# Nearest-neighbour upsampling: a fourth load for the last rows, and a first group copied by one engine

## The chip, the cores and the metric

The kernel runs on one core of a Trainium2 chip. The metric is the device time in microseconds (us) of one execution. A profile is one execution recorded by the hardware profiler; its span runs from the first instruction of the program to the last event that it records.

## The reference

```python
batch, channels, h, w = x.shape            # 16, 64, 64, 64, float32
new_h, new_w = (h * scale_factor, w * scale_factor)   # scale_factor = 2
...
        src_i = i // scale_factor
        src_j = j // scale_factor
        result[:, :, i, j] = x[:, :, src_i, src_j].copy()
```

Every input element is written four times: twice along the row and in two neighbouring rows. 16.78 MB are read, 67.11 MB are written, and nothing is computed.

## The kernel before

The 65,536 input rows of 64 numbers are spread over 128 partitions, 512 neighbouring rows in each (R = 512). One input row is 256 bytes in a partition, and becomes 256 numbers, 1 KB, of output (two output rows of 128).

One tile, `mem`, holds everything: 79 x 256 numbers of free room at its front, and behind it the whole input, `xt` (512 x 64 numbers). The groups of output rows are built in this tile and overwrite input that is used up: groups with an even number at the tile's start, groups with an odd number so that they end where the group's own input rows begin. Two groups that follow each other do not overlap, and a group overwrites the one two before it, or input already expanded. So the copies of a group wait for the store of the group two before it to land.

**Loads** (lines 192 to 195). Three DMAs issued on SyncE (SP), cut at rows 0, 32, 288 and 512 of each partition: 8 KB, 64 KB and 56 KB in each partition. `begin_before_barrier` (lines 13 to 33) takes the first `EARLY` instructions of SP in the body, which are these loads, and puts them ahead of the barrier that all engines pass at the start.

**Groups** (lines 204 to 216). `rows` gives nine groups of 54, 38, 54, 61, 54, 63, 63, 63 and 62 input rows. For each group VectorE (DVE in the profile, line 213) expands the first `kv` rows with a broadcast copy, ScalarE (ACT, line 214) the rest, and SP issues one store of the whole group (line 215), which waits for both:

```python
        kv = k - 1 if n == 0 else k * 5 // 8 & ~1
        nc.vector.tensor_copy(out=u[:, :kv], in_=expanded(r0, r0 + kv))
        nc.scalar.copy(out=u[:, kv:], in_=expanded(r0 + kv, r0 + k))
        nc.sync.dma_start(out=op[:, r0 : r0 + k, :], in_=u)
```

For groups 1 to 8 `kv` is five eighths of the rows, rounded down to an even number (22, 32, 38, 32, 38, 38, 38, 38). For group 0 it is all rows but one, 53, and ACT copies the one row. Group 0 needs rows 0 to 53, so loads 1 and 2. The second group overwrites input of group 0 and waits for VectorE's first copy.

All DMAs, loads and stores, are issued by SP on one hardware queue. Each increments one of eight semaphores, given out in turn; with three loads and nine stores there are twelve DMAs. `close_early` (lines 80 to 151) rewrites the end of the program: GpSimd waits for all semaphores but that of the last store and clears them, and SP waits for the last store alone. The loads are numbered 1 to 4 below, the groups and their stores 0 to 8.

Of the kernel before, what the change touches and what calls it, by code (L numbers as in the profile page):

```python
# [6 lines left out]

EARLY = 3  # L10


def begin_before_barrier(nc):
# [5 lines left out]
    sp = mybir.EngineType.SP  # L19
    loads = [i for i in body.instructions if i.engine == sp][:EARLY]  # L20
    for load in loads:
# [132 lines left out]
@with_exitstack  # L154
def kernel(
    ctx: ExitStack,
    tc: tile.TileContext,
    x: bass.AP,
    scale_factor: int,
    out: bass.AP,  # L160
):
    nc = tc.nc
    nc.at_finalize(begin_before_barrier)
    nc.at_finalize(close_early)
    P = nc.NUM_PARTITIONS
    s = int(scale_factor)
    B, C, H, W = x.shape
    R = B * C * H // P
    fdt = x.dtype

    xp = x.rearrange("b c h w -> (b c h) w").rearrange("(p r) w -> p r w", p=P)
    op = out.rearrange("b c (h hd) w -> (b c h) (hd w)", hd=s).rearrange(
        "(p r) w -> p r w", p=P
    )

    rows = [54, 38, 54, 61, 54, 63, 63, 63, 62]
    GROW = s * s
    FREE = 79
    WF = FREE * GROW * W
    assert sum(rows) == R
    mem_pool = ctx.enter_context(tc.tile_pool(name="mem", bufs=1))
    mem = mem_pool.tile([P, WF + R * W], fdt, name="mem")
    xt = mem[:, WF:].rearrange("p (r w) -> p r w", r=R)

    HEAD = 32
    cuts = [0, HEAD, R // 2 + HEAD, R]
    for lo, hi in zip(cuts, cuts[1:]):
        nc.sync.dma_start(out=xt[:, lo:hi], in_=xp[:, lo:hi])  # L195

    def expanded(r0, r1):
        return (
            xt[:, r0:r1].unsqueeze(2).unsqueeze(4).to_broadcast([P, r1 - r0, s, W, s])
        )  # L200

    r0 = 0
    before = (0, 0)
    for n, k in enumerate(rows):
        size = k * GROW * W
        at = 0 if n % 2 == 0 else WF + r0 * W - size
        assert at >= before[1] or at + size <= before[0]
        before = (at, at + size)
        u = mem[:, at : at + size].rearrange(
            "p (k a w b) -> p k a w b", k=k, a=s, w=W  # L210
        )
        kv = k - 1 if n == 0 else k * 5 // 8 & ~1
        nc.vector.tensor_copy(out=u[:, :kv], in_=expanded(r0, r0 + kv))  # L213
        nc.scalar.copy(out=u[:, kv:], in_=expanded(r0 + kv, r0 + k))  # L214
        nc.sync.dma_start(out=op[:, r0 : r0 + k, :], in_=u)  # L215
        r0 += k

# [34 lines left out]
```

## Time and profile before

| what | value |
|---|---|
| median of 3 runs | 197.13 us (197.12 to 197.15) |
| the profiled execution's own time | 196.92 us |
| its span | 195.6 us |
| busy: VectorE, ACT | 52.3 us, 42.1 us |
| DMA queue q1, share of 16 engines | 99.2% |
| bytes moved | 83.89 MB, mean 429 GB/s |
| VectorE's first copy, 53 rows | starts at 24.11 us, 14.29 us long |
| store 0 issued, landed | 38.48 us, 57.30 us |
| store 1 issued | 42.11 us |

In the profile's lines L213 is line 213 of the kernel before. A line of groups reads: line, engine, operation, output and input with shapes (partitions x elements), count, then the busy time in us and the mean duration of one in ns, then the idle time of that engine just before these instructions and what ended it. A line of the timeline reads: start, length, engine, line, operation, and in square brackets the idle time before it and what it waited for. The chain that ended last follows the work back from the last instruction, at each step to what released it. A row of DMA issues gives the count, the KB of one and the median time from issue to landing.

### The profile page before, as it was taken

The page shows a single profiled execution, that of the slowest core. Times are in us where ns is not written, and L with a number is a line of the kernel's source. Part 1 is how long each engine was busy: PE and PEld are TensorE (multiplying, and loading weights), DVE is VectorE, ACT ScalarE, POOL GpSimd, SP SyncE. Part 2 cuts the span into 40 slices and gives each one's busy share as a digit, 9 for nine tenths or more (in the row PEclk, how much of TensorE's full clock was granted, in tenths as well). Part 3 has the DMA queues.
Part 4 walks back from the last instruction along what each step waited for, and adds up shares of the span by engine and source line. Part 5 has one row for each costly group of instructions (what it writes and reads, how often), then busy time and mean ns, then how long its engine had stood idle before and what let it go on. Part 6 is the DMA issues. An engine that isn't in the chain of part 4 may idle for free.

```text
span 195.6 us, 102 instructions
## 1 busy us (share of the span) xinstructions
DVE 52.3 (27%) x9; ACT 42.1 (21%) x10; POOL 0.2 (0%) x4
## 2 busy tenths in 40 slices
DVE  0000099940026091053008204500540073000000
ACT  2000000160029700059500004970000073000000
POOL 0000000000000000000000000000000000000000
DMA  9999989889899989999999899999999999999994
GB/s 429 429 429 429 402 375 563 375 362 543 362 436 390 555 362 418 486 409 409 409 420 532 362 531 433 422 422 422 422 422 422 422 422 422 422 435 545 467 428 208
DMA packets 1728, 83.89 MB, mean 429 GB/s; under 512 B 192, under 2 KB 192, under 8 KB 192
## 3 DMA queue, kind: packets, MB, share of 16 engines
q1 hardware_dynamic: 1728, 83.89, 99.2%
HBM read 16.78 MB, written 67.11 MB: 429 GB/s over the span
## 4 chain that ended last, share of the span: by engine, by line
DMA 65%; ACT 11%; DVE 7%; SPq 0%; issue 0%; DVEq 0%; ACTq 0%
DMA out_dram<-mem 53%; DMA mem<-in_x_dram 12%; ACT mem L214 11%; DVE mem L213 7%; SPq L195 0%; DVEq L213 0%; ACTq L214 0%; SPq L215 0%
## 5 line engine op out<-in xcount | busy, mean ns | idle before, releaser
L213 DVE COPY mem<-mem 128x9728 f32<-128x9728 f32 (+3 forms) x9 | 52.3, 5818 | 110.9 <-DMA out_dram<-mem 86.8
L214 ACT COPY mem<-mem 128x6400 f32<-128x6400 f32 (+5 forms) x9 | 40.8, 4530 | 119.4 <-DMA out_dram<-mem 84.2
L214 ACT ACT_TABLE_LOAD x1 | 1.3, 1283 | 1.7 <-PEq L233 1.7
L233 POOL MEMSET const-bfloat16-1.0<- 128x1 bf16 x1 | 0.1, 102 | 0.0
L233 POOL MEMSET const-uint8-127<- 128x1 uint8 x1 | 0.1, 102 | 0.0
L233 POOL MEMSET const-float32-1.0<- 128x1 f32 x1 | 0.1, 99 | 0.0
L233 POOL MEMSET const-float32-0.0<- 128x1 f32 x1 | 0.1, 98 | 0.2 <-issue 0.2
## 6 DMA issues: line engine op xcount, KB each, us to landing
out_dram<-mem SPq DMA_DIRECT2D x3, 8064.0 KB, 32.4
out_dram<-mem SPq DMA_DIRECT2D x3, 6912.0 KB, 22.9
out_dram<-mem SPq DMA_DIRECT2D x1, 7936.0 KB, 32.3
out_dram<-mem SPq DMA_DIRECT2D x1, 7808.0 KB, 29.3
mem<-in_x_dram SPq DMA_DIRECT2D x1, 7168.0 KB, 40.1
out_dram<-mem SPq DMA_DIRECT2D x1, 4864.0 KB, 26.7
mem<-in_x_dram SPq DMA_DIRECT2D x1, 1024.0 KB, 4.7
mem<-in_x_dram SPq DMA_DIRECT2D x1, 23.6
```

Source lines behind the costliest of these rows:

```text
L213: nc.vector.tensor_copy(out=u[:, :kv], in_=expanded(r0, r0 + kv))
L214: nc.scalar.copy(out=u[:, kv:], in_=expanded(r0 + kv, r0 + k))
L233: nc = _bacc.Bacc("TRN2", target_bir_lowering=False, num_devices=1)
```

## The change

```diff
-EARLY = 3
+EARLY = 4
...
     HEAD = 32
-    cuts = [0, HEAD, R // 2 + HEAD, R]
+    TAIL = 8
+    cuts = [0, HEAD, R // 2 + HEAD, R - TAIL, R]
     for lo, hi in zip(cuts, cuts[1:]):
         nc.sync.dma_start(out=xt[:, lo:hi], in_=xp[:, lo:hi])
...
-        kv = k - 1 if n == 0 else k * 5 // 8 & ~1
+        kv = k if n == 0 else k * 5 // 8 & ~1
         nc.vector.tensor_copy(out=u[:, :kv], in_=expanded(r0, r0 + kv))
-        nc.scalar.copy(out=u[:, kv:], in_=expanded(r0 + kv, r0 + k))
+        if kv < k:
+            nc.scalar.copy(out=u[:, kv:], in_=expanded(r0 + kv, r0 + k))
         nc.sync.dma_start(out=op[:, r0 : r0 + k, :], in_=u)
```

Load 3 ends eight rows earlier (rows 288 to 503, 54 KB in each partition), and a fourth load brings rows 504 to 511 (2 KB in each partition). It too goes ahead of the barrier. Group 0 is copied by VectorE alone, 54 rows; ACT has no part in it, and store 0 waits for VectorE only. The rest is as before; the thirteenth DMA shifts by one which of the eight semaphores each store uses. In the built program ACT's table load, which stood ahead of its first copy without a wait, now stands behind a wait for loads 1 and 2.

## The prediction

> **What bounds the kernel now.** I read the page's share of busy time and its DMA rows first, then the chain that ended last, then the copies by form, and last the starts of single copies in the timeline. From the page:
>
> ```profile
> span 195.6 us, 102 instructions
> DVE 52.3 (27%) x9; ACT 42.1 (21%) x10; POOL 0.2 (0%) x4
> ...
> DMA packets 1728, 83.89 MB, mean 429 GB/s; under 512 B 192, under 2 KB 192, under 8 KB 192
> ...
> q1 hardware_dynamic: 1728, 83.89, 99.2%
> ```
>
> No engine that computes is busy for a third of the span; the one DMA queue keeps its 16 engines busy for 99.2% of it. What is left is 0.8% x 195.6 = 1.6 us, and the table by stages puts 1.0 us of that before the first packet (nothing moves between 0 and 1.00 us). So the transfers bound the kernel, and the end can move by one of two ways only: the engines get more or less to do, or they run dry somewhere. The packets also say how a DMA is cut: 1728 packets over 12 DMAs are 144 each, 9 for each of 16 engines, and the 192 under 512 B are 16 a DMA, so an engine has 8 data packets (one for each of 8 partitions) and one short one.
>
> The stretch that the change touches, from the chain of waits (start, length, what):
>
> ```profile
> 0.42 23.59 DMA mem<-in_x_dram
> ...
> 24.11 14.30 DVE mem L213
> 38.41 0.02 issue
> 38.42 0.02 SPq L215
> 38.44 0.04 issue
> 38.48 18.82 DMA out_dram<-mem
> 57.30 0.02 issue
> 57.33 4.89 ACT mem L214
> ```
>
> Load 2 lands at 24.01, VectorE copies the first group for 14.30 us, and store 0 is issued at 38.48. This looks like a path that VectorE sets. It is not: the third load was issued at 0.9 (first and last issue of L195: 0.0 to 0.9) and its row says
>
> ```profile
> mem<-in_x_dram SPq DMA_DIRECT2D x1, 7168.0 KB, 40.1
> ```
>
> so it was still landing until 0.9 + 40.1 = 41.0, 2.5 us after store 0 had been issued. The chain follows the instruction that released a wait; it does not see that the engines had other bytes to move meanwhile.
>
> Whether they ran dry is read from the rate. Each later group starts on VectorE when an earlier store has landed:
>
> ```profile
> 57.40 4.43 DVE L213 COPY mem<-mem 128x8192 f32<-128x8192 f32 x1 [16.00 <-DMA out_dram<-mem]
> 68.89 5.23 DVE L213 COPY mem<-mem 128x9728 f32<-128x9728 f32 x1 [7.07 <-DMA out_dram<-mem]
> 85.18 4.43 DVE L213 COPY mem<-mem 128x8192 f32<-128x8192 f32 x1 [11.06 <-DMA out_dram<-mem]
> 103.61 5.23 DVE L213 COPY mem<-mem 128x9728 f32<-128x9728 f32 x1 [14.00 <-DMA out_dram<-mem]
> 119.94 5.23 DVE L213 COPY mem<-mem 128x9728 f32<-128x9728 f32 x1 [11.11 <-DMA out_dram<-mem]
> 138.95 5.23 DVE L213 COPY mem<-mem 128x9728 f32<-128x9728 f32 x1 [13.78 <-DMA out_dram<-mem]
> 157.93 5.23 DVE L213 COPY mem<-mem 128x9728 f32<-128x9728 f32 x1 [13.75 <-DMA out_dram<-mem]
> ```
>
> The steps between them are the times of the stores of 38, 54, 61, 54, 63 and 63 rows: 11.49, 16.29, 18.43, 16.33, 19.01 and 18.98 us. From 38 to 63 rows: (18.995 - 11.49) / 25 = 0.3002 us a row (1 KB in each partition), and 11.49 - 38 x 0.3002 = 0.08 us left as the fixed part of one DMA. The 54 and 61 rows then come out at 16.29 and 18.39, so the fit holds to 0.05 us. Loads go by the same numbers, counted in KB a partition: load 3 has 56, so 16.81 + 0.08 = 16.89, against 41.0 - 24.01 = 17.0. And store 0 took 57.30 - 41.0 = 16.3 from the landing of load 3, against 16.29: at the switch from loads to stores no more than 0.05 us of pause is to be found.
>
> **The change part by part.**
>
> First copy. The forms by line price it:
>
> ```profile
> L213 DVE COPY mem<-mem 128x9728 f32<-128x9728 f32 x5 | 26.1, 5227 | 59.7 <-DMA out_dram<-mem 59.7
> ...
> L213 DVE COPY mem<-mem 128x13568 f32<-128x13568 f32 x1 | 14.3, 14285 | 24.1 <-DMA mem<-in_x_dram 24.1
> ...
> L213 DVE COPY mem<-mem 128x8192 f32<-128x8192 f32 x2 | 8.9, 4428 | 27.1 <-DMA out_dram<-mem 27.1
> ```
>
> The 53-row copy took 1.053 ns an element, the 38- and 32-row ones 0.537 and 0.541: half. All VectorE copies but the first have an even number of rows, so the new one of 54 is priced by these: (5227 - 4428) / 1536 = 0.520 ns an element, and 5227 + 4096 x 0.520 = 7358 ns. Store 0 is then issued at 24.11 + 7.36 + 0.08 (the gap seen in the chain) = 31.55 in place of 38.48, 6.9 us earlier. What is late next is the engines' own queue: loads 3 and 4 keep them until 41.1, and the store waits behind these. I cost the earlier issue at **nothing**; at most it takes the 0.05 us of pause. The rule by which an odd count is slow is itself open: the Trainium skill (VectorE: DVE Perf Modes, "What auto-detection actually checks") gives the fast mode also to odd outermost counts that are equal in source and destination, and the 53-row copy, equal on both sides as written, ran at 1.053 ns; this case's trace does not bear that half out.
>
> ACT. Its 256-element copy goes (405 ns, at 24.03, beside VectorE's 14.3 us: nothing on the path). In the new order of instructions the table load (1283 ns) stands behind a wait for loads 1 and 2, so it moves from 1.72 to about 24.0 and ends at 25.3; the first ACT copy that needs it starts at 31.55, so 6.2 us cover it. Were the cover gone, store 1 would be later by up to 1.3 us and store 0 not at all. The copy of 4096 elements (3606 ns) then ends at 35.2, store 1 is issued there in place of 42.11, and it waits behind store 0. Group 2 overwrites group 0's buffer and waits for store 0 to land, at 57.4 as before.
>
> The fourth load. SP issues one more DMA, 0.43 us (L195: 372 to 432 ns each), ahead of its barrier. Loads 1 to 3 are issued before it and don't move. Behind it on SP stands only the barrier, which releases VectorE and ACT at about 2.1 in place of 1.7; both then wait for load 2 until 24.0, so 21 us cover it. The stores on the same queue come at 31.5 or later. The first readers of its 8 rows are in the last group, at 157.9, over 110 us after its landing. On the DMA engines: the bytes are the same, 54 + 2 KB a partition in place of 56; one more fixed part is added, 0.08 us by the fit. A DMA of 2 KB a partition does not occur before, so both ends: the fit's scatter, with half or double the fixed part, gives -0.05 (the step of 54 rows varies by 0.04) to +0.15; far above stands load 1, 8 KB a partition and nothing ahead of it: landed 4.7 after issue, 8 x 0.3002 = 2.4 of it for bytes, 2.3 us besides. I take **0.08**, since load 4 is issued at 1.3, with 39 us of transfers ahead of it, like loads 2 and 3, which show no such start-up (load 2: 24.0 - 4.7 = 19.3, by the fit 64 x 0.3002 + 0.08 = 19.29).
>
> A rule that speaks against this edit: the Trainium skill (DMA: Bandwidth & Descriptors, "Anatomy of one DMA") fits 2.0 us of fixed time to every DMA, which would make this one 2.6 us and the sum +2.0. The trace bears that size out for load 1, alone at the front, and not for DMAs queued behind others.
>
> Sum, against the profiled execution: 195.59 + 0.08 - 0 = 195.67 of span. Around its span it has 196.92 - 195.59 = 1.33 us, so 197.00; the median of the runs, 197.13, is 0.21 above that execution, so **197.21**, +0.04%. Measurements of this kernel tell no change from up to 0.2% (0.39 us), so this is no change.
>
> **Rivals.**
>
> Slower: the fourth load's short packets stall the queue. Mechanism: between load 3 and store 0 each engine has eight 2 KB reads; if the start-up that load 1 shows is paid again there, because small reads run out before the next are ready, it is not hidden: everything behind is later by up to 2.3 us, 197.13 + 2.3 = 199.4. It decides from the point where the eight packets cost (0.39 - 0.08) / 8 = 40 ns each more than their bytes. For it: the smallest packets of data so far are 8 KB, and those are the ones with a slow front (262 and 213 GB/s from 1.0 to 2.0, 442 at 2.0 to 2.5). Against: the rate at 2.0 to 2.5 is full while those 8 KB packets still run, and the queue is filled 39 us ahead.
>
> Faster: the switch at 41.0 gains. If store 0's descriptors, ready 7 us sooner, take away the 0.05 us of pause, if load 3 (17.0 against 16.89) gets back the 0.1 us that it may lose beside the slow copy, and the extra load costs nothing, it is 197.13 - 0.15 = 197.0. More than that has no idle time in the trace to come from.
>
> Not doing what it says: the 54-row copy stays at 1.053 ns an element, 14.6 us. Store 0 is issued at 38.8, still 2.3 us before the loads have landed: 197.2 again. The first copy's length is no lever here either way.
>
> **How the numbers follow.** Forecast 0.74, slower 0.13 (spread from 197.5 to 199.4), faster 0.08 (a quarter of it beyond 0.2%, for an idle stretch that I don't see), copy stays slow 0.05. Faster by over 0.2%: 0.02, slower by over 0.2%: 0.13, within: 0.85. The range takes in the faster rival and both ends of the fit, 197.0 below, and above goes to 197.6, the near part of the slower rival; about 1.5 in 10 is left out, nearly all above.
>
> **What would show it.** Right: the first DVE copy at 7.4 us, store 0 issued near 31.6 but taking about 25.8 to land (18.8 before), at 57.4; store 1 landing near 68.9; every later start of a copy 0.0 to 0.15 later than before; the queue's share still 99%. Wrong: store 0 landing later than 57.7 (small reads cost), or earlier than 57.2 (there was a pause that I missed); a span that moves without this landing moving would put the cause at the front or the end, where I see none.

## The result, and the profile after

The changed kernel took 198.62 us (median of 4 runs, 198.40 to 198.79) beside 197.12 for the kernel before, run next to it: 1.0076 times, 95% interval 1.0064 to 1.0089. It is slower by 1.5 us; 197.21 had been forecast, with a range of 197.0 to 197.6. The profiled execution took 198.79, with a span of 197.5; it is the longest of the four runs, and its span is 1.9 us above that of before.

The page of the changed kernel, the lines that answer to those of before:

```profile
span 197.5 us, 102 instructions
DVE 45.3 (23%) x9; ACT 41.6 (21%) x9; POOL 0.2 (0%) x4
...
DMA packets 1872, 83.89 MB, mean 425 GB/s; under 512 B 208, under 2 KB 208, under 8 KB 336
...
q1 hardware_dynamic: 1872, 83.89, 99.2%
...
mem<-in_x_dram SPq DMA_DIRECT2D x1, 6912.0 KB, 41.3
out_dram<-mem SPq DMA_DIRECT2D x1, 4864.0 KB, 35.5
mem<-in_x_dram SPq DMA_DIRECT2D x1, 1024.0 KB, 4.7
mem<-in_x_dram SPq DMA_DIRECT2D x1, 256.0 KB, 41.5
```

The row of 6912 KB is load 3, now 54 KB in each partition. The queue is 99.2% busy, exactly as before, though it needed 1.9 us more of span for the same bytes. A busy share tells that packets are under way, not that they move at full rate; the mean rate does, 425 GB/s against 429.

The chain of waits of the changed kernel (start, length, what), and its first copy among the groups by form:

```profile
0.42 23.61 DMA mem<-in_x_dram
...
24.13 7.37 DVE mem L214
31.50 0.02 issue
31.52 27.64 DMA out_dram<-mem
59.16 0.02 issue
59.18 4.89 ACT mem L216
```

```profile
L214 DVE COPY mem<-mem 128x13824 f32<-128x13824 f32 x1 | 7.4, 7360 | 24.1 <-DMA mem<-in_x_dram 24.1
```

VectorE's part came out as worked: 7360 ns, store 0 issued at 31.52. But store 0 landed at 59.16 in place of 57.30, 1.86 us later. From there on the stages keep their lengths: the DVE copies that wait for stores start at 59.25, 70.76, 87.03 and so on to 159.80, each 1.8 to 1.9 us behind before. So the loss lies between 24.0 (load 2, landed as before) and 59.2. The trace's record of single packets, which no view here shows, places it: the 16 last packets of load 3, one on each engine, start at 37.5 to 38.0 and take 3.1 to 4.0 us, where load 3's other packets of that size (55,296 bytes) take 2.04. The 2 KB packets of load 4 behind them take 84 ns in the median, what their bytes ask for.

I use one measure below: from load 2's landing to store 0's landing. It is 33.3 us before and 35.1 in the changed kernel. "Excess" is the time by which the packets around the switch from loads to stores run longer than packets of their size do in the rest of the trace, as a mean per engine: 0.02 us before, 1.53 in the changed kernel. A landing waits for the slowest engine, so the two measures need not agree.

### The profile page after: what moved, and what is told of

Its sections match the earlier page's. It is cut to its first block, busy times and chain, and to the rows that moved or that the text cites. A ratio compares the mean times of both kernels' runs of the same rounds, so it can differ in the third digit from the quotient of the medians.

```text
span 197.5 us, 102 instructions
## 1 busy us (share of the span) xinstructions
DVE 45.3 (23%) x9; ACT 41.6 (21%) x9; POOL 0.2 (0%) x4
## 3 DMA queue, kind: packets, MB, share of 16 engines
q1 hardware_dynamic: 1872, 83.89, 99.2%
## 4 chain that ended last, share of the span: by engine, by line
DMA 69%; ACT 10%; DVE 4%; SPq 0%; issue 0%; DVEq 0%
DMA out_dram<-mem 57%; DMA mem<-in_x_dram 12%; ACT mem L216 10%; DVE mem L214 4%; SPq L196 0%; DVEq L214 0%
## 5 line engine op out<-in xcount | busy, mean ns | idle before, releaser
L214 DVE COPY mem<-mem 128x9728 f32<-128x9728 f32 (+3 forms) x9 | 45.3, 5048 | 119.7 <-DMA out_dram<-mem 95.5
L216 ACT COPY mem<-mem 128x6400 f32<-128x6400 f32 (+4 forms) x8 | 40.4, 5045 | 99.3 <-DMA out_dram<-mem 93.1
## 6 DMA issues: line engine op xcount, KB each, us to landing
mem<-in_x_dram SPq DMA_DIRECT2D x1, 6912.0 KB, 41.3
mem<-in_x_dram SPq DMA_DIRECT2D x1, 256.0 KB, 41.5
```

## The experiments

Each is an edit of the changed kernel. HBM is the main memory, which holds the input and the output; `mem` lies in the on-chip memory. "Three loads" means `EARLY = 3` and the cuts of before.

**Three loads, early store** (e1)

```diff
-EARLY = 4
+EARLY = 3
-    cuts = [0, HEAD, R // 2 + HEAD, R - TAIL, R]
+    cuts = [0, HEAD, R // 2 + HEAD, R]
```

> The changed kernel without its fourth load: three loads as before, group 0 still copied by VectorE alone in 7.4 us, store 0 issued near 31.5. Theory A (small reads: the eight 2 KB reads of each engine, all at the same place of rows 128 KB apart, are slow in memory): load 3 lands at 41.0, store 0 at 57.4, time 197.1. Theory B (early store: stores that already wait in the queue when the loads end make the switch from reading to writing cost 1.8 us): load 3 lands near 42.8, store 0 near 59.1, time 198.6. Theory C (a short load just ahead of a store, both needed): 197.1.

**Four loads, the copy of before** (e2)

```diff
-        kv = k if n == 0 else k * 5 // 8 & ~1
+        kv = k - 1 if n == 0 else k * 5 // 8 & ~1
```

> The fourth load alone: group 0 copied as before, 53 rows on VectorE (14.3 us) and one on ACT, store 0 issued at 38.5. Theory A: the last packets of load 3 run to near 41 to 42 as in the changed kernel, store 0 lands near 59.1, time 198.6. Theory B: store 0 lands at 57.4, time 197.2. Theory C: near 198.6, if a store issued 2.5 us ahead of the switch is early enough.

**The short load second** (e3)

```diff
-    for lo, hi in zip(cuts, cuts[1:]):
+    parts = list(zip(cuts, cuts[1:]))
+    for lo, hi in [parts[0], parts[3], parts[1], parts[2]]:
```

> The changed kernel with the 2 KB load second in the order instead of last: loads of rows 0 to 31, 504 to 511, 32 to 287, 288 to 503. Theory A: the cost moves with the short load; the load of rows 32 to 287 lands near 24.0 + 0.7 + 1.8 = 26.5, time 198.6. Theory B: that load lands at 24.7, the cost stays at the switch near 41, time 198.6. Theory C: no short load stands ahead of a store, that load lands at 24.7, store 0 at 57.4, time 197.2.

**The short load from one block of HBM** (e4; the last 8 output rows of each partition are other data)

```diff
-    for lo, hi in zip(cuts, cuts[1:]):
+    for lo, hi in zip(cuts[:3], cuts[1:4]):
         nc.sync.dma_start(out=xt[:, lo:hi], in_=xp[:, lo:hi])
+    flat = x.rearrange("b c h w -> (b c h) w")[R * 64 : R * 64 + P * TAIL]
+    nc.sync.dma_start(out=xt[:, hi:], in_=flat.rearrange("(p r) w -> p r w", p=P))
```

> The changed kernel, but the fourth load fetches one contiguous block of 256 KB of the input (row 32768 on) in place of the last 8 rows of each partition, 2 KB a partition, so its reads lie 2 KB apart in place of 128 KB; the last 8 output rows of each partition are other data. Theory A: the cost goes, load 4 lands near 41.1, store 0 at 57.4, time 197.2. Theories B and C: as the changed kernel, store 0 near 59.1, 198.6.

Measured against the kernel before, with the ratio and its interval in brackets: e1 198.41 us (1.0054, 1.0037 to 1.0071); e2 197.24 (0.9995, 0.9986 to 1.0005); e3 198.37 (1.0051, 1.0036 to 1.0066); e4 198.42 (1.0054, 1.0039 to 1.0069). The early store alone is slow, the fourth load alone is not, and neither the place of the short load nor where it reads takes the loss away. Theory B holds; A falls as the main cause, and C falls. The row of load 3 and the step of store 0 in the chain of e2, which has the same four loads as the changed kernel:

```profile
mem<-in_x_dram SPq DMA_DIRECT2D x1, 6912.0 KB, 39.6
```

```profile
38.60 18.87 DMA out_dram<-mem
```

So the same load 3 lands 39.6 us after its issue with the late store, and 41.3 us after it with the early one. The chain of e1, and its row of load 3:

```profile
0.43 24.02 DMA mem<-in_x_dram
...
24.56 7.37 DVE mem L214
31.93 0.02 issue
31.95 26.80 DMA out_dram<-mem
```

```profile
mem<-in_x_dram SPq DMA_DIRECT2D x1, 7168.0 KB, 41.5
```

Load 2 landed at 24.45 there (its first load started slowly), store 0 at 58.75: 34.3 us, 1.0 more than before. Load 3 stands at 41.5 in place of 40.1; 0.4 us of that is the late front. The excess is 1.05 us, again on the last packet of load 3 on every engine.

**ACT copies group 0 alone** (e5, three loads)

```diff
-        kv = k if n == 0 else k * 5 // 8 & ~1
-        nc.vector.tensor_copy(out=u[:, :kv], in_=expanded(r0, r0 + kv))
+        kv = 0 if n == 0 else k * 5 // 8 & ~1
+        if kv:
+            nc.vector.tensor_copy(out=u[:, :kv], in_=expanded(r0, r0 + kv))
```

> Three loads, group 0 copied by ACT alone (about 11.7 us after its table load), so store 0 is issued near 37.1: about 1.3 us before the last packets of load 3 start (38.3 in the trace of before), where before issues it at 38.5. Theory B1 (it is enough that the store waits in the queue when the last load packet starts): the last packets of load 3 take about 1 us longer, load 3 lands near 42, store 0 near 58.5, time 198.2 to 198.5. Theory B2 (the cost grows with the time that the store waits): well under 0.4 us of cost, 197.2 to 197.5. If neither, the cause is not the store in the queue but the fast copy on VectorE: 197.1.

**Store 1 late** (e6, three loads)

```diff
-        kv = k if n == 0 else k * 5 // 8 & ~1
+        kv = k if n == 0 else k - 1 if n == 1 else k * 5 // 8 & ~1
```

> Three loads, store 0 at 31.5 as in e1_three_loads, but group 1 copied slowly (37 rows on VectorE in one odd copy, 10 us, one row on ACT), so store 1 is issued near 41.7, behind the switch, in place of 35. Theory B: one waiting store is enough, load 3 lands near 42, 198.4 as e1_three_loads. Theory D (it takes two stores waiting, four DMAs in the queue, such as a limit of the queue): load 3 lands at 41.0, time 197.1.

**A load behind store 0** (e7, `EARLY = 3`, `TAIL = 32`; the first three loads go ahead as before)

```diff
         nc.sync.dma_start(out=op[:, r0 : r0 + k, :], in_=u)
+        if n == 0:
+            nc.sync.dma_start(out=xt[:, R - TAIL :], in_=xp[:, R - TAIL :])
```

> The changed kernel's copy, and the last 32 rows of each partition (8 KB) loaded by a DMA that is issued right behind store 0: the queue holds load 3 (48 KB), store 0, load 4, store 1, so it switches from loads to stores twice. If every such switch with a waiting store costs about 1 us: load 3 lands near 39.6 (38.5 without cost), store 0 near 56, store 1 near 71 (68.9 without any cost), time about 199.4. If only the first switch costs: 198.4. If a switch from store to load costs as well, more.

**64 rows in the fourth load** (e8)

```diff
-    TAIL = 8
+    TAIL = 64
```

> The changed kernel with 64 rows (16 KB a partition) in the fourth load and 40 KB in load 3. It tells where the lost time falls. If it falls on the packet that ends at the switch (theory B, place 1), load 3 lands without delay near 36.2 + 0.1 and load 4 about 1 us late, near 42.2. If it falls at a fixed distance of 16 KB or more ahead of the stores (place 2, as on the last packet of load 3 in the changed kernel), packets further forward in load 4 or the last of load 3 are long. The time is 198.4 to 198.6 either way.

Measured against the kernel before: e5 198.08 us (1.0033, 1.0022 to 1.0045), excess 1.10; e6 198.34 (1.0043, 1.0028 to 1.0058), excess 1.19; e7 199.80 (1.0113, 1.0098 to 1.0128); e8 198.42 (1.0047, 1.0030 to 1.0064), excess 1.18. So VectorE's fast copy of group 0 is not the cause (e5 does without it), and one waiting store is enough (e6 issued the second at 41.7). A store issued 1.3 us earlier than before's has as much excess as one issued 7 us earlier (e5's was issued at 37.14; its time is lower than e6's, but the intervals overlap). B2 and D fall. In e7 the packets at the first switch from loads to stores have an excess of 1.05 us and those around the second 0.95. Of the second, 0.73 lies on the last packets of store 0 and only 0.21 on load 4's. Store 0 landed at 57.87, where I had expected about 56. So a second price is paid, but whether load 4 waiting behind store 0 brings it on, or store 1 waiting behind load 4, is not separated here. e8's short packets show when it is paid. Its stages (us, then DVE, ACT and POOL busy, clock, DMA share, GB/s):

```profile
30.00:36.00 6.00, 4.75 (x2) 3.61 (x1) 0.00 (x0) 1.00 0.86 371
38.50:40.50 2.00, 0.00 (x0) 0.00 (x0) 0.00 (x0) 1.00 1.12 262
```

From 38.5 to 40.5, ahead of the switch, the engines are fully busy at 262 GB/s: the 16 KB packets there take up to 1.3 us, where their bytes ask for 0.61. (A packet's bytes count where it starts, so single stages stray; this one holds several packets of each engine.) Place 2 was right: the loss begins some 3 us ahead of the switch and is mostly over by the last packets, which take 0.71 us in the mean.

**Store 0 on ACT's queue** (e9, three loads)

```diff
-        nc.sync.dma_start(out=op[:, r0 : r0 + k, :], in_=u)
+        (nc.scalar if n == 0 else nc.sync).dma_start(
+            out=op[:, r0 : r0 + k, :], in_=u
+        )
```

> Three loads and the fast copy, but store 0 is issued by ACT on its own hardware queue near 31.6, so its packets don't stand behind load 3's and may run between them. Theory P (while an engine still writes a load into the on-chip memory, the reading of a store out of it, ahead of time, slows both): loads and store 0 overlap for far longer than at one switch, load 3 lands much later than the share of the bytes explains, and the whole loses more than the 1 us of e1_three_loads, 199 to 202. Theory Q (only the hand-over inside one queue costs): no hand-over is left between load 3 and store 0, 197.1 to 197.4.

201.99 us (1.0260, 1.0239 to 1.0281). The packets of load 3 and store 0 together lost 2.45 us for each engine. On each engine 1.6 of it, in the mean, fell on one packet of load 3, which ran just before the store's first packet. After that the engines took packets of the two queues in turn, from 37.4 to 48.1 us, and lost 0.1 to 0.3 us a packet in the mean, less towards the end. The rest of the time is another matter: store 0 shared the engines and landed late, the copies of group 2 waited for it, and the engines ran dry:

```profile
70.00:71.00 1.00, 1.00 (x1) 1.00 (x1) 0.00 (x0) 1.00 0.10 39
71.00:72.00 1.00, 1.00 (x1) 1.00 (x1) 0.00 (x0) 1.00 0.00 0
```

The time is in theory P's range, but its reason is not borne out: most of the loss came when the store came in, and little while the two ran side by side. Theory Q falls, since that loss came with no hand-over left inside one queue.

**The changed kernel again** (e10, no edit)

> The changed kernel once more, beside the others of this call and a fresh profile: does its fourth load cost anything on top of the early store? The changed kernel stood at 1.0076 of before, e1_three_loads (no fourth load) at 1.0054 and e4_tail_contiguous at 1.0054, with intervals that touch. If the 2 KB reads cost by themselves 0.4 us: again 1.007 to 1.008, and store 0 lands near 59.1. If the difference was scatter: 1.0055, store 0 near 58.8.

198.57 us (1.0075, 1.0058 to 1.0092), store 0 at 59.01, excess 1.42. The early-store variants without short, spread reads at the end of the loads have 0.87 to 1.19 (e1, e3 to e6, e8, and e11 below). So these reads, behind load 3 and just ahead of a waiting store, seem to cost 0.3 to 0.5 us more; e2 shows that without the waiting store they cost nothing (excess 0.01). The intervals of the times touch, so this rests on two profiles.

**Store 0 between 37.1 and 38.5** (e11: pieces ending at 45, 46, 54; e14: at 49, 50, 54; three loads)

```diff
-        nc.vector.tensor_copy(out=u[:, :kv], in_=expanded(r0, r0 + kv))
+        for a, b in ((0, 45), (45, 46), (46, 54)) if n == 0 else ((0, kv),):
+            nc.vector.tensor_copy(out=u[:, a:b], in_=expanded(r0 + a, r0 + b))
```

> Three loads; VectorE copies group 0 in three pieces of 45, 1 and 8 rows (two of them odd), so store 0 is issued near 37.8: between e5_act_alone (37.1, load 3 landed about 1 us late) and before (38.5, no delay). If the cost is all or nothing, set by whether the store is queued when load 3's last packets start (38.1 to 38.5): load 3 lands at 41.0 or at 42, and with the about 0.6 us that an issue takes to reach the engines the first is expected, or engines divided. If it grows with the lead: about half, load 3 at 41.5, 197.5.

> As e11_store0_at_38 with pieces of 49, 1 and 4 rows, store 0 issued near 38.1 (e11: 37.6 and 0.9 us lost on load 3's last packets; before: 38.5 and nothing). If the loss is what an engine reads ahead of the store while it still has load bytes to come, it shrinks with the time left: about 0.4 us, 197.5. If it is all or nothing: 0.9 us and 198, or nothing and 197.1, or some engines with and some without.

e11 197.95 us (1.0046, 1.0031 to 1.0061), e14 197.23 (0.9993, 0.9984 to 1.0002). The issue of store 0 and its length to landing, from the chains of e11 and of e14:

```profile
37.59 20.79 DMA out_dram<-mem
```

```profile
38.26 19.41 DMA out_dram<-mem
```

With three loads, the excess goes with the time of issue like this:

| store 0 issued at | excess, us |
|---|---|
| 31.63 and 31.95 (e6, e1) | 1.19 and 1.05 |
| 37.14 (e5) | 1.10 |
| 37.59 (e11) | 0.87 |
| 38.26 (e14) | 0.18 |
| 38.48 (before) | 0.02 |

It is close to 38.5 minus the time of issue, and no more than about 1.1 to 1.2: neither all or nothing nor growing without a limit. In these runs the last packets of load 3 start at 38.2 to 38.5 (means over the engines), so the loss is about the time by which the issue precedes them, up to that limit. The kernel before issued its store just late enough to pay nothing.

**A copy inside HBM between load 3 and store 0** (e12, three loads; the output is whole, the last store overwrites these rows)

```diff
+    nc.sync.dma_start(out=op[:, R - 16 :, :], in_=x.rearrange(
+        "b c h w -> (b c h) w").rearrange("(p r) w -> p (r w)", p=P)[:, : 16 * s * s * W])
```

> The copy and early store of the changed kernel, three loads, and as a fourth early DMA a copy inside HBM of 16 KB a partition from the input to the last output rows, which the last store overwrites later: 2.1 MB more, 16 x 0.30 = 4.9 us if it goes at the rate of the others. It stands between load 3 and store 0, so what is read ahead behind load 3 comes from HBM and not from the on-chip memory. Theory P: load 3 lands without delay near 41.0, and since the HBM copy writes nothing on chip store 0 starts without loss too; total about 197.1 + 4.9 = 202.0. Theory S (any change of the kind of transfer with a waiting successor costs): load 3 lands near 42, total 203 or more.

**The same with a late store** (e13)

```diff
         nc.vector.tensor_copy(out=u[:, :kv], in_=expanded(r0, r0 + kv))
+        if n == 0:
+            nc.vector.tensor_copy(out=u[:, :45], in_=expanded(r0, r0 + 45))
```

> As e12_hbm_between (a copy inside HBM of 16 KB a partition between load 3 and store 0), but VectorE copies 45 of the 54 rows of group 0 a second time in an odd, slow copy (12.2 us), so store 0 is issued near 43.7 in place of 31.5, about 2.2 us before the HBM copy should end (45.9). Theory S (the waiting store slows what is ahead of it, whatever that writes): the HBM copy lands near 46.0 in place of 47.3, store 0 near 62.3, time about 202.1. If the HBM copy is slow by itself: it lands at 47.3 again, store 0 at 63.7, 203.4.

e12 took 203.36 us (1.0321, 1.0306 to 1.0336), e13 204.55 (1.0367, 1.0350 to 1.0385). The rows of load 3 and of the HBM copy in e12:

```profile
mem<-in_x_dram SPq DMA_DIRECT2D x1, 7168.0 KB, 40.1
...
out_dram<-in_x_dram SPq DMA_DIRECT2D x1, 2048.0 KB, 46.0
```

and of the HBM copy in e13:

```profile
out_dram<-in_x_dram SPq DMA_DIRECT2D x1, 2048.0 KB, 44.7
```

With the HBM copy behind it, load 3 lands without delay (40.1, as before). The HBM copy is now what stands ahead of the store: its packets have an excess of 1.14 us in e12 and 0.06 in e13, so it is not slow by itself. Theory P, in which the store's reading disturbs a load's writing into the on-chip memory, falls, since the HBM copy writes nothing there. Theory S as I put it falls for load 3. What is left is that a waiting store slows what is read from HBM ahead of it, wherever that is written. A mixing of reads and writes in HBM as such is not it either: the copy of e13 does both, and its 16 KB packets took 0.61 us, no more than e8's 16 KB loads ahead of the loss. In e13 I missed the time: VectorE put a copy of group 1 ahead, store 0 was issued at 46.7, after the HBM copy had landed, and the engines had nothing to move (stages as above):

```profile
45.00:46.00 1.00, 1.00 (x1) 0.00 (x0) 0.00 (x0) 1.00 0.05 16
46.00:47.00 1.00, 0.68 (x1) 0.29 (x1) 0.00 (x0) 1.00 0.00 0
```

That pause of about 2.2 us, less the 1.1 that was saved, is why it is slower than e12. No variant beat the kernel before; e2 and e14 equal it.

## Why the prediction was wrong

**The bound was right.** The DMA engines set the end, VectorE's 6.9 us gained nothing, and the later stages kept their lengths. The copy's price (7358 ns worked, 7360 measured), the hidden table load of ACT and the hidden fourth issue on SP were right as well.

**The step that failed** is "I cost the earlier issue at **nothing**". It supposed that a store waiting behind a load costs the load nothing, since engines work a queue in order. The trace of before could not show otherwise: load follows load or store follows store everywhere but at one switch, and there the store came in at 38.5, when it cost 0.02 us. Measured: 1.05 us of excess and about 1.0 us of time for the early store alone (e1). Under it lies the sentence that the end can move "by one of two ways only", more work for the engines or engines that run dry. The third way was missing: the same bytes moved more slowly. I read 99% as proof that nothing was to be lost; a packet that takes 3.5 us in place of 2.0 is busy all the time.

**The fourth load** at 0.08 us held by itself (e2: 33.3 us from load 2 to store 0, as before). The rule of 2.0 us for every DMA that the prediction set against it from the Trainium skill (DMA: Bandwidth & Descriptors, "Anatomy of one DMA") is measured there on DMAs issued from GpSimd, while the DMAs here are issued by SP. But with the early store the load seems to add 0.3 to 0.5 us. The edits were priced one by one; together they cost more.

**The slower rival** had the sign and a span that holds the time (197.5 to 199.4), by the wrong mechanism: short reads in the queue. My own sign for it, store 0 landing later than 57.7, came up (59.16) and would have confirmed it falsely: that landing moves with either cause. Only the packets of load 3, long ahead of the short ones, and e1 tell them apart.

**What causes it, as far as shown.** Shown: the early store costs the time (e1 beside before, the changed kernel beside e2), and it does so by lengthening the HBM reads ahead of it over the last 3 us or so before the switch, by 1.1 to 1.2 us at most (1.4 to 1.5 with the short reads between), by less the later it is issued. The long packets at the end of store 0 in e7 do not fit HBM reads alone, and stay open. Argued only: each engine begins to read the store out of the on-chip memory while it still has reads from HBM to finish, the two share the engine's reading, and this stops when some buffer is full; by an estimate, 1.1 us at an engine's 27 GB/s (55,296 bytes in 2.04 us) would be some 30 KB. The Trainium skill (DMA: Bandwidth & Descriptors, "Two DMAs through the same engine are not ordered") says that an engine's read and write sides are separate queues and that descriptors start in order but overlap; that allows such reading ahead and gives no price for it. Why what was read ahead is not won back later, and why short reads add to it, stays open.

## What to carry to other kernels

Where the DMA engines bound the time, as here, issuing a store earlier than they can take it gained nothing and cost about 1 us behind loads that still ran. The store cost nothing when it was issued about when the loads' last packets started, 38.5 us here; earlier lost up to 1.2 us, and a store issued after the transfers ahead of it had ended left a pause of 2.2 us (e13). Times between these were not tried. Read rates and single packets beside the busy share, and price edits that meet in one queue together.

## What the hardware showed beyond that

- A copy inside HBM of 2.1 MB, queued behind loads, moved at the rate of loads: it landed 5.0 us after load 3 in e13 (46.1 against 41.1), where 4.9 had been worked out.
- VectorE copies with an odd number of rows ran at one element in 1.05 ns wherever they were tried (53, 49, 45 and 37 rows: 14,285, 13,220, 12,153 and 10,019 ns), and even ones of 22 rows and more at about half of that (54 rows: 7,360 ns).
- A store on another engine's queue is not kept behind the loads: in e9 load 3 and store 0 shared the 16 engines, and load 3 landed 49.7 us after its issue (40.1 before).
